# Tokens laid out by residue class in a decoder block: the dilated attention groups read side by side, the dense group regroups its blocks

## The chip, the cores and the metric

The kernel runs on one core of a Trainium2 chip. Its engines are TensorE (PE; its weight loads are listed as PEld), VectorE (DVE), ScalarE (ACT), GpSimd (POOL) and SyncE (SP), which issues most DMAs. Each engine works through its own instructions in program order. The metric is the device time of one execution in microseconds (us); the kernel before has a median of 969.9 us over three runs (968.4 to 971.77).

## The reference

One decoder block on 512 tokens of width 1024, in float32. `mod` comes from a condition vector `c` through `w_ada` (9216 outputs).

```python
u = modulate(rmsnorm(h, g_norm_ffn1), sh1, sc1)
h = h + 0.5 * gt1 * swiglu(u, w_ffn1_in, w_ffn1_out)
u = modulate(rmsnorm(h, g_norm_mix), sh2, sc2)
h = h + gt2 * token_mixing(u, ...)
u = modulate(rmsnorm(h, g_norm_ffn2), sh3, sc3)
h = h + 0.5 * gt3 * swiglu(u, w_ffn2_in, w_ffn2_out)
return rmsnorm(h, g_final)

def token_mixing(u, ...):
    p, q, k, v, gate_logits = split(u @ w_in)
    y_pool = multiscale_pool(p)      # trailing means over 2, 4, 8, 16 tokens, minus the token
    q, k = apply_rope(q), apply_rope(k)
    # three groups of 4 heads, head width 64: (window 128, dilation 1), (512, 4), (2048, 16);
    # token t attends to t - j * dilation, on banded blocks of 128 queries;
    # the groups are combined by a softmax over their log denominators
    y_attn = ...
    return (g_pool * (y_pool @ w_pool_branch) + g_attn * (y_attn @ w_attn_branch)) @ w_out
```

With dilation 4, tokens 4i + c for one c form a sequence of 128 that never meets the other three. Dilation 16 stays within the same class, with a mask (`(q - k) % 4 == 0`) inside it.

## The kernel before

All activations lie transposed: the 128 partitions hold features, the free dimension holds the 512 tokens, and a tensor of width 1024 is eight tiles of 128 x 512. Float32 products are made from three products of split operands: a weight chunk in `raw` (512 KB, loaded by SP, line 295) is rounded by ACT to `whi` (line 377), DVE makes the rest `wlo` (line 389), and the activations are kept as `UH` and `UL`. `take()` hands out split chunks, `split` and `look` make them ahead of use, and three `raw` buffers go round. `bg()` is work put between: one 128 x 1024 slice of `w_ada` in a buffer `xs` (loaded by SP, line 440) is multiplied with the condition and summed by DVE (line 448). It fetches up to two slices ahead, when it is called.

The change lies in `mix()`, the token mixing, from about 340 to 510 us of the span. The order on each engine is that in which the code is written; waits are set by the data. The steps, in their order:

1. q and k of group 0 (dilation 1) are made in four banks. `rope_two` copies them with signs (ACT, line 1409), moves 32-partition pieces with eight DMAs on SP (line 1412) and multiplies with the cosines (DVE, line 1414). `rope_b` adds the part with the sines (lines 1419, 1420).
2. v of group 0: four blocks n of 128 tokens, 24 matmuls each (lines 1675 to 1677), copied by ACT to `v1` (line 1678). Between them stand a weight split, its next load, `rope_b` and `bg()`. With n = 2 one `bg()` is called, with n = 3 two.
3. q and k of groups 1 and 2: eight `mm_tile`s of 24 matmuls (lines 421 to 423). At k = 5 of each stand, on PE, attention steps for group 0: the values (line 1508), the transposes of the probabilities (line 1490, `at_turn`) of the tile before, and new scores (line 1457). `at_exp` takes the scores with a mask and a maximum on DVE (lines 1473, 1475) and the exponential on ACT (line 1478). `rope_a` writes q and k of these groups sorted by class (`(i c) -> p c i`): DVE reads the bank and the cosines with a step of four elements (line 1402), `rope_b` reads the sine part so (line 1420).
4. Two tiles for the pooling mixer; `pool_diff` works them on POOL (lines 1583 to 1592).
5. v of groups 1 and 2, by class c: 24 matmuls of 128 tokens of the class against 512 columns. `by_class` gathers the class's columns of `UH` into `uc` or `v1` (ACT, line 1720); of `UL` the stationary operand is read with a step of four (line 1768). DVE copies the bank to `v23` (line 1769); the values of the dilated blocks (line 1508) read it.
6. The statistics of the dilated groups go through DRAM (`at_swap`, lines 1518, 1519) to the order of group 0; `at_merge`, `at_fT` and the rest combine the groups.

The functions that the diff touches, with the line numbers of the profile:

Of the kernel before, what the change touches and what calls it, by code (L numbers as in the profile page):

```python
# [14 lines left out]
P = 128  # L15
T = 512
# [149 lines left out]
class Kernel:  # L166
# [1226 lines left out]
    def rope_a(self, bank, dst, hp, classes, t, w):  # L1393


        nc = self.nc
        nc.scalar.activation(t, bank, AF.Copy, scale=self.sign)
# [4 lines left out]
        nc.vector.tensor_tensor(dst[:, hp * T:hp * T + T].rearrange("p (c i) -> p c i", c=classes), by(bank), by(self.cos),  # L1402
                                op=OP.mult)

    def rope_two(self, banks, dst, t, w):

        nc = self.nc
        for hp in range(2):
            nc.scalar.activation(t[:, hp * T:hp * T + T], banks[hp], AF.Copy, scale=self.sign)
        for i in range(4):  # L1410
            o = i ^ 1
            nc.sync.dma_start(w[32 * o:32 * o + 32], t[32 * i:32 * i + 32])
# [3 lines left out]
    def rope_b(self, dst, hp, classes, w):  # L1416
        v = self.nc.vector
        d = dst[:, hp * T:hp * T + T].rearrange("p (c i) -> p c i", c=classes)
        v.tensor_tensor(w, w, self.sin, op=OP.mult)
        v.tensor_tensor(d, d, w.rearrange("p (i c) -> p c i", c=classes), op=OP.add)  # L1420
# [17 lines left out]
    def at_tokens(self, u):  # L1438
        kind, n, hp = u
        return (1, 2) if kind else (0,), slice(n * P, n * P + P)  # L1440

    def at_scores(self, u):


        kind, n, hp = u
        nc = self.nc
        gs, toks = self.at_tokens(u)
        for i, g in enumerate(gs):
            for h in range(2):
                rows = slice(64 * h, 64 * h + 64)  # L1450
                q, k = (x[g][rows, hp * T:hp * T + T] for x in (self.qt, self.kt))
                if kind:
                    o, ks = slice(i * P, i * P + P), toks
                else:
                    o, ks = (slice(0, 2 * P), slice((n - 1) * P, (n + 1) * P)) if n else (slice(P, 2 * P), toks)
                S = self.bS[h][:, 2 * P * hp:2 * P * hp + 2 * P]
                nc.tensor.matmul(S[:, o], q[:, toks], k[:, ks], start=True, stop=True, skip_group_check=True)
# [41 lines left out]
    def at_values(self, u):  # L1499

        kind, n, hp = u
        pt = self.probT.pop(u)
        first = 0 if kind or n else 1
        for j in range(first, 2):
            for h in range(2):
                hc = 64 * (2 * hp + h)
                x = self.v23[:, n, 256 * j + hc:256 * j + hc + 64] if kind else self.v1[:, n - 1 + j, hc:hc + 64]
                self.nc.tensor.matmul(self.bO[64 * h:64 * h + 64, P * hp:P * hp + P], x,
                                      pt[:, (2 * h + j) * P:(2 * h + j + 1) * P], start=j == first, stop=j == 1,
                                      skip_group_check=True)  # L1510
        if hp == 1:
            o = self.o23.rearrange("p a (i c) -> p a c i", c=4)[:, :, n] if kind else self.o1[:, :, n * P:n * P + P]
            self.nc.vector.tensor_copy(o, self.bO[:, :256].rearrange("p (a i) -> p a i", a=2))

    def at_swap(self):

        nc = self.nc
        nc.sync.dma_start(self.scr.rearrange("(i c) f -> i c f", c=4), self.st)
        nc.sync.dma_start(self.stn, self.scr.rearrange("(n i) f -> i n f", n=4))
# [19 lines left out]
    def at_fT(self, bank):  # L1539
# [5 lines left out]
        nc.scalar.activation(self.fT[:8], bank[:8], AF.Copy)  # L1545
        v.tensor_tensor(self.fT[32:40], bank[:8], self.fT[:8], op=OP.subtract)
# [21 lines left out]
    def pool_diff(self, t, bank):  # L1568
# [8 lines left out]
        nc.scalar.activation(p[:, 16:], bank, AF.Copy)  # L1577
# [8 lines left out]
        for half, w in ((0, w0), (1, 2 * w0)):  # L1586
# [3 lines left out]
            g.tensor_scalar(d[rows, 16:], s[rows, 32:], 1.0 / w, None, op0=OP.mult)  # L1590
            g.tensor_tensor(d[rows, :16], s[rows, 16:32], ic, op=OP.mult)
            g.tensor_tensor(d[rows], d[rows], p[rows, 16:], op=OP.subtract)
# [17 lines left out]
    def mix(self):  # L1610
# [14 lines left out]
        with tc.tile_pool(name="rt", bufs=1) as self.rt, tc.tile_pool(name="aw", bufs=2) as self.aw:  # L1625
# [10 lines left out]
            masks = ma.tile([P, 3 * P], F32, name="masks")  # L1636
            nc.sync.dma_start(masks, self.a["cst"][:, 163:547])
            self.mask = [masks[:, :256], masks[:, 128:]]
# [25 lines left out]
            self.look(2)  # L1664
            for n in range(4):
# [7 lines left out]
                for k in range(KT):  # L1673
                    hi, lo = w[k]
                    M(b[:, :256], self.UH[k][:, ts], hi, start=k == 0, stop=False)
                    M(b[:, :256], self.UH[k][:, ts], lo, start=False, stop=False)
                    M(b[:, :256], self.UL[k][:, ts], hi, start=False, stop=k == KT - 1)
                nc.scalar.activation(self.v1[:, n, :], b[:, :256], AF.Copy)
                for i in ((), (0, 1), (2, 3), ())[n]:
                    self.rope_b(*to[i], 1, sw[i])  # L1680
# [22 lines left out]
            for g in (1, 2):  # L1703
                for dst in (self.qt[g], self.kt[g]):
                    for hp in range(2):
# [3 lines left out]
                        self.rope_a(b, dst, hp, 4, *rt)  # L1709

                        rest = [(6, lambda dst=dst, hp=hp, w=rt[1]: self.rope_b(dst, hp, 4, w))]
# [3 lines left out]
            uc = {}  # L1715

            def by_class(c):

                uc[c] = (ma if c % 2 else mp).tile([P, D], F32R, name="v1" if c % 2 else "uc")
                nc.scalar.activation(uc[c].rearrange("p (k i) -> p k i", k=KT),  # L1720
                                     self.UHv.rearrange("p (k i c) -> p c k i", k=KT, c=4)[:, c], AF.Copy)

            b = self.mm_tile(hooks([], rest + [(3, self.bg), (6, lambda: by_class(0))]))
# [15 lines left out]
            b = self.mm_tile(hooks(g23[0], [(2, lambda: by_class(1)), (3, u["copies"]), (4, u["adds"]), (7, self.bg)]))  # L1739
# [18 lines left out]
            for c in range(4):  # L1758
                mid = [lambda c=c: by_class(c + 1)] if c in (1, 2) else []
                hk = hooks(g23[c + 1] if c < 3 else [], [(k, f) for n, k, f in beside if n == c], mid)  # L1760
                b = self.nb()
                for k in range(KT):
                    for f in hk.get(k, ()):
                        f()
                    (hi, lo), uh = w[k], uc[c][:, k * P:k * P + P]
                    M(b, uh, hi, start=k == 0, stop=False)
                    M(b, uh, lo, start=False, stop=False)
                    M(b, self.UL[k][:, c::4], hi, start=False, stop=k == KT - 1)
# [368 lines left out]
def constants():  # L2137
# [4 lines left out]
    for t in range(2):  # L2142
        for half in range(2):
# [4 lines left out]
    q, k = i[:, None], i[None, :]  # L2148
    return np.concatenate([invf[i % 32][:, None], sign[:, None], np.zeros((P, 1), np.float32), cnt,
                           np.eye(P, dtype=np.float32),  # L2150
                           neg(k >= q), neg(k <= q), neg((k <= q) & ((q - k) % 4 == 0))], axis=1)


def lay_inputs(x, c, positions, w_ada, b_ada, g_norm_ffn1, w_ffn1_in, w_ffn1_out, g_norm_mix, w_in, w_pool,
# [7 lines left out]
    for g in range(4):  # L2162
# [3 lines left out]
        "xT": A(x)[0].T.reshape(KT, P, T).transpose(1, 0, 2).reshape(P, KT * T),  # L2166
        "c": A(c),
        "pos": A(positions),
# [25 lines left out]
```

## Time and profile before

| | |
|---|---|
| median of three runs | 969.9 us |
| span of the profiled execution, first to last instruction | 967.1 us |
| what lies around the span, median less span | 2.8 us |
| PE busy, of the span | 956.6 us (99%) |
| DVE, ACT, POOL busy | 846.8, 545.2, 82.8 us |
| mean granted TensorE clock | 0.998 |
| PE busy from 340 to 520 us | 179.60 of 180.00 us |

The 2.8 us hold the launch around a span and the difference between two executions. A timeline row gives start and duration in us from the span's start, then engine (SPq is SP issuing), line, operation, what is written and read, how many; in square brackets the idle time before it and what ended that. A row for a DMA tells how long SP took to issue, not how long the transfer took; its landing is told by the DMA view.

### The profile page before, as it was taken

To read this page: it belongs to the slowest core of one execution; us is meant where nothing else is said; L and a number is where in the kernel's file an instruction comes from. 1 tells how busy PE (TensorE), PEld (TensorE's weight loads), DVE (VectorE), ACT (ScalarE), POOL (GpSimd) and SP (SyncE) were. 2 spreads that over 40 slices of the span, in tenths; PEclk is the share of its full clock that TensorE was granted. 3 is DMA by queue.
4 is the path that set the end of the run, shared out by engine and by line. 5 is a ranking of instruction groups with operands and counts; after the bars stand their busy time and mean duration, and the time that the engine had idled before them with its cause. 6 is when DMAs were issued, how large, how long until landed. Compare 5 with 4: busy or idle time off the path is not lost.

```text
span 967.1 us, 18132 instructions
## 1 busy us (share of the span) xinstructions
PE 956.6 (99%) x7296; PEld 900.7 (93%) x7296; DVE 846.8 (88%) x1237; ACT 545.2 (56%) x817; POOL 82.8 (9%) x90
## 2 busy tenths in 40 slices
PE   9999999999999999999999999999999999999996
PEld 7888999999999899788899998998999999999996
DVE  7989999899999789898888777888899988989885
ACT  5443666665755553446665543465665657556565
POOL 0000110101010000006500000000001100010002
PEclk9999999999999999999999999999999999999999
DMA  9857785786768547767266537723757666665622
GB/s 354 282 179 256 187 246 159 201 213 153 218 175 254 167 145 226 247 192 221 54 163 186 133 108 231 243 63 111 181 153 194 163 167 175 163 165 136 179 69 88
DMA packets 53144, 174.12 MB, mean 180 GB/s; under 512 B 7105, under 2 KB 9921, under 8 KB 52802
## 3 DMA queue, kind: packets, MB, share of 16 engines
q1 hardware_dynamic: 43984, 141.23, 44.3%
q0 software_dynamic: 8496, 31.20, 17.9%
q8 instruction: 57, 0.93, 0.4%
q10 hardware_dynamic: 578, 0.53, 0.2%
q14 instruction: 29, 0.24, 0.1%
HBM read 135.29 MB, written 2.24 MB: 142 GB/s over the span
## 4 chain that ended last, share of the span: by engine, by line
PE 86%; DVE 8%; issue 2%; DMA 2%; ACT 1%; POOL 0%; POOLq 0%; ACTq 0%; DVEq 0%
PE bank L751 12%; PE bank L749 12%; PE bank L750 12%; PE bank L421 8%; PE bank L422 8%; PE bank L423 8%; PE bank L1110 4%; PE bank L1108 4%; PE bank L1109 4%; DVE wlo L389 2%; PE bank L2120 2%; PE bank L2124 2%; PE bank L2122 1%; DMA v<-wada 1%; DMA cs<-wada 1%
## 5 line engine op out<-in xcount | busy, mean ns | idle before, releaser
L389 DVE TENSOR_TENSOR wlo<-raw,whi 128x1024 fp32r<-128x1024 f32 (+3 forms) x150 | 166.0, 1115 | 35.0 <-ACT whi L377 34.9
L749 PE MATMUL bank<-UH,whi 128*128 128x256 f32 x672 | 185.5, 276 | 0.0
L750 PE MATMUL bank<-UL,whi 128*128 128x256 f32 x672 | 185.5, 276 | 0.0
L751 PE MATMUL bank<-UH,wlo 128*128 128x256 f32 x672 | 185.5, 276 | 0.0
L389 DVE TENSOR_TENSOR wlo<-X,whi 128x1024 fp32r<-128x1024 f32 (+3 forms) x133 | 142.0, 1080 | 17.6 <-ACT whi L377 17.5
L377 ACT ACTIVATE whi<-raw 128x1024 fp32r<-128x1024 f32 (+3 forms) x150 | 142.5, 963 | 21.2 <-DMA raw<-wf1o 7.8
L377 ACT ACTIVATE whi<-X 128x1024 fp32r<-128x1024 f32 (+3 forms) x133 | 123.1, 946 | 52.0 <-DVE X L312 46.8
L749 PEld LDWEIGHTS bank<-UH,whi 128*128 128x128 f32 x672 | 126.1, 188 | 0.1
L750 PEld LDWEIGHTS bank<-UL,whi 128*128 128x128 f32 x672 | 126.1, 188 | 0.0
L751 PEld LDWEIGHTS bank<-UH,wlo 128*128 128x128 f32 x672 | 126.1, 188 | 0.0
L749 PE MATMUL bank<-SH,whi 128*128 128x256 f32 x408 | 112.6, 276 | 0.0
L751 PE MATMUL bank<-SH,wlo 128*128 128x256 f32 x408 | 112.6, 276 | 0.0
L750 PE MATMUL bank<-SL,whi 128*128 128x256 f32 x408 | 112.6, 276 | 0.0
L421 PE MATMUL bank<-UH,whi 128*128 128x512 f32 (+1 forms) x272 | 92.9, 341 | 0.0
L422 PE MATMUL bank<-UL,whi 128*128 128x512 f32 (+1 forms) x272 | 91.8, 338 | 0.0
L423 PE MATMUL bank<-UH,wlo 128*128 128x512 f32 (+1 forms) x272 | 91.6, 337 | 0.0
L750 PEld LDWEIGHTS bank<-SL,whi 128*128 128x128 f32 x408 | 76.6, 188 | 0.0
L749 PEld LDWEIGHTS bank<-SH,whi 128*128 128x128 f32 x408 | 76.6, 188 | 0.0
L751 PEld LDWEIGHTS bank<-SH,wlo 128*128 128x128 f32 x408 | 76.6, 188 | 0.0
L1109 PE MATMUL bank<-HK,whi 128*128 128x256 f32 x224 | 61.8, 276 | 0.0
L1110 PE MATMUL bank<-HI,wlo 128*128 128x256 f32 x224 | 61.8, 276 | 0.0
L1108 PE MATMUL bank<-HI,whi 128*128 128x256 f32 x224 | 61.8, 276 | 0.0
(411 smaller groups left out, 2421.3 us busy)
## 6 DMA issues: line engine op xcount, KB each, us to landing
raw<-wmix SPq DMA_DIRECT2D x44, 512.0 KB, 4.2
raw<-wf1i SPq DMA_DIRECT2D x32, 512.0 KB, 5.8
raw<-wf2i SPq DMA_DIRECT2D x30, 512.0 KB, 4.3
ada<-wada SPq DMA_DIRECT2D x23, 512.0 KB, 5.6
X<-raw POOLq DMA_DIRECT2D x23, 512.0 KB, 6.0
xs<-wada SPq DMA_DIRECT2D x17, 512.0 KB, 5.3
X<-wf2i SPq DMA_DIRECT2D x14, 512.0 KB, 4.6
X<-wf1i SPq DMA_DIRECT2D x11, 512.0 KB, 4.5
```

What stands on the lines that cost most here:

```text
L377: self.nc.scalar.activation(self.hi[:, y], r[:, x], AF.Copy)
L389: self.nc.vector.tensor_tensor(self.lo[:, y], r[:, x], self.hi[:, y], op=OP.subtract)
L421: M(ps, hi, uh, start=start, stop=False)
L422: M(ps, hi, ul, start=False, stop=False)
L423: M(ps, lo, uh, start=False, stop=stop)
L749: M(o, hi, uh, start=start and p == 0 and k == 0, stop=False, skip_group_check=True)
L750: M(o, hi, ul, start=False, stop=False, skip_group_check=True)
L751: M(o, lo, uh, start=False, stop=k == 3, skip_group_check=True)
L1108: M(o, hi, uh, start=start and m % 2 == 0 and k == 0, stop=False, skip_group_check=True)
L1109: M(o, hi, ul, start=False, stop=False, skip_group_check=True)
L1110: M(o, lo, uh, start=False, stop=k == 1, skip_group_check=True)
L2120: M(b, hi, self.UH[k], start=k == 0, stop=False)
```

## The change

The host lays tokens in the order of class: position 128c + i holds token 4i + c, in `x`, in `positions` and, back again, in the result. Everything that is per token stays as it was. The dilated groups find their class as 128 neighbouring columns, so `rope_a`, `rope_b`, the class products and `o23` work on contiguous columns and `by_class` goes. What depends on token order has to undo the layout: group 0 writes q and k in blocks of 128 consecutive tokens, `(n c i)`, each block again sorted by class (new masks follow that order); its v is first copied to `vc` (in the buffer `uc`) and moved to `v1` by 16 DMAs of 32 partitions; its output, the statistics and the pooling mixer are reordered with access patterns.

```diff
-    def rope_a(self, bank, dst, hp, classes, t, w):
+    def rope_a(self, bank, dst, hp, t, w):
...
-        by = lambda x: x.rearrange("p (i c) -> p c i", c=classes)
-        nc.vector.tensor_tensor(dst[:, hp * T:hp * T + T].rearrange("p (c i) -> p c i", c=classes), by(bank), by(self.cos),
-                                op=OP.mult)
+        nc.vector.tensor_tensor(dst[:, hp * T:hp * T + T], bank, self.cos, op=OP.mult)
...
         for hp in range(2):          # rope_two
-            nc.vector.tensor_tensor(dst[:, hp * T:hp * T + T], banks[hp], self.cos, op=OP.mult)
+            by = lambda x: x.rearrange("p (c n i) -> p n c i", c=4, n=4)
+            o = dst[:, hp * T:hp * T + T].rearrange("p (n c i) -> p n c i", n=4, c=4)
+            nc.vector.tensor_tensor(o, by(banks[hp]), by(self.cos), op=OP.mult)
...
+    def rope_b(self, dst, hp, w, near=False):
         v.tensor_tensor(w, w, self.sin, op=OP.mult)
+        if near:
+            d = d.rearrange("p (n c i) -> p n c i", n=4, c=4)
+            w = w.rearrange("p (c n i) -> p n c i", c=4, n=4)
+        v.tensor_tensor(d, d, w, op=OP.add)
...
+            if kind:                 # at_values
+                self.nc.vector.tensor_copy(self.o23[:, :, n * P:n * P + P], b.rearrange("p (a i) -> p a i", a=2))
+            else:
+                self.nc.vector.tensor_copy(self.o1.rearrange("p a (c n i) -> p n a c i", c=4, n=4)[:, n],
+                                           b.rearrange("p (a c i) -> p a c i", a=2, c=4))
...
-        nc.sync.dma_start(self.scr.rearrange("(i c) f -> i c f", c=4), self.st)
-        nc.sync.dma_start(self.stn, self.scr.rearrange("(n i) f -> i n f", n=4))
+        nc.sync.dma_start(self.scr.rearrange("(c i) f -> i c f", c=4), self.st)
+        for c in range(4):
+            nc.sync.dma_start(self.stn[32 * c:32 * c + 32], self.scr.rearrange("(c n i) f -> c i n f", c=4, n=4)[c])
...
-        nc.scalar.activation(p[:, 16:], bank, AF.Copy)          # pool_diff
+        nc.scalar.activation(p[:, 16:].rearrange("p (i c) -> p c i", c=4), bank.rearrange("p (c i) -> p c i", c=4), AF.Copy)
...
+            o, by = d[rows].rearrange("p (c i) -> p c i", c=4), lambda x: x.rearrange("p (i c) -> p c i", c=4)
+            g.tensor_scalar(o[:, :, 4:], by(s[rows, 32:]), 1.0 / w, None, op0=OP.mult)
+            g.tensor_tensor(o[:, :, :4], by(s[rows, 16:32]), by(ic), op=OP.mult)
+            g.tensor_tensor(o, o, by(p[rows, 16:]), op=OP.subtract)
...
+            vc = mp.tile([P, D], F32, name="uc")
             for n in range(4):
...
-                nc.scalar.activation(self.v1[:, n, :], b[:, :256], AF.Copy)
+                nc.scalar.activation(vc[:, n * 256:n * 256 + 256], b[:, :256], AF.Copy)
+                for i in range(4):
+                    nc.sync.dma_start(self.v1[32 * n:32 * n + 32, i, :], vc[32 * i:32 * i + 32, n * 256:n * 256 + 256])
                 for i in ((), (0, 1), (2, 3), ())[n]:
-                    self.rope_b(*to[i], 1, sw[i])
+                    self.rope_b(*to[i], sw[i], True)
...
-            def by_class(c):
-                uc[c] = (ma if c % 2 else mp).tile([P, D], F32R, name="v1" if c % 2 else "uc")
-                nc.scalar.activation(uc[c].rearrange("p (k i) -> p k i", k=KT),
-                                     self.UHv.rearrange("p (k i c) -> p c k i", k=KT, c=4)[:, c], AF.Copy)
...
-                    (hi, lo), uh = w[k], uc[c][:, k * P:k * P + P]
+                    (hi, lo), uh, ul = w[k], *(x[k][:, c * P:c * P + P] for x in (self.UH, self.UL))
                     M(b, uh, hi, start=k == 0, stop=False)
                     M(b, uh, lo, start=False, stop=False)
-                    M(b, self.UL[k][:, c::4], hi, start=False, stop=k == KT - 1)
+                    M(b, ul, hi, start=False, stop=k == KT - 1)
```

The number and order of the matmuls on PE stay the same. The instructions move at two places.

SP in step 2, from the last piece moves of `rope_two` to the first of `rope_a`: `xs` is a slice of `w_ada`, `raw` a weight chunk, `q`, `k` and `rt` are rope pieces. Before:

```order
L1412 DMA k_3518<-v_3520 32x1024 x4
L440 DMA xs<-wada 128x1024
L295 DMA raw_63<-wmix 128x1024
L295 DMA raw_64<-wmix 128x1024
L440 DMA xs<-wada 128x1024
L295 DMA raw_65<-wmix 128x1024
L440 DMA xs<-wada 128x1024 x3
L1400 DMA rt_3976<-tr 32x512 x4
```

Loads alone stand between the two groups of moves.

And the same stretch of SP after, with `v_3519` for `v1`:

```order
L1410 DMA k_3518<-v_3520 32x1024 x4
L440 DMA xs<-wada 128x1024
L1687 DMA v_3519<-uc 32x256 x4
L295 DMA raw_63<-wmix 128x1024
L1687 DMA v_3519<-uc 32x256 x4
L295 DMA raw_64<-wmix 128x1024
L1687 DMA v_3519<-uc 32x256 x4
L440 DMA xs<-wada 128x1024
L295 DMA raw_65<-wmix 128x1024
L1687 DMA v_3519<-uc 32x256 x4
L440 DMA xs<-wada 128x1024 x3
L1400 DMA rt_3993<-tr 32x512 x4
```

Twelve moves of `v1` pieces stand ahead of the second single `xs` load, eight ahead of the second `raw` load, sixteen ahead of the last three `xs` loads.

DVE at the same place does not change its order. From the last `rope_b` of group 0 to the first maxima of the scores, after:

```order
L1419 TENSOR_TENSOR k_3518<-k_3518,cs 128x512
L1423 TENSOR_TENSOR k_3516<-k_3516,k_3518 128x512
L448 SCALAR_TENSOR_TENSOR xs,mod<-xs,cond 128x1024
L389 TENSOR_TENSOR wlo<-raw_65,whi 128x1024
L448 SCALAR_TENSOR_TENSOR xs,mod<-xs,cond 128x1024
L459 TENSOR_TENSOR mod<-mod,vecs 128x8
L448 SCALAR_TENSOR_TENSOR xs,mod<-xs,cond 128x1024
L389 TENSOR_TENSOR wlo<-raw_63,whi 128x1024
L1472 ISA prob,m_3527<-bank_93,masks 128x128
L1472 ISA m_3527 128x1
```

Three products with slices of `w_ada` (line 448) stand ahead of the first maximum (line 1472, 1473 before); the third of them reads the slice of that second single `xs` load.

ACT loses the four gathers of `UH`. In steps 4 and 5, before:

```order
L377 ACTIVATE whi<-raw_65 128x1024
L1720 ACTIVATE uc<-UH 128x1024
L1577 ACTIVATE tr<-bank_91 128x512
L377 ACTIVATE whi<-raw_63 128x1024
L1720 ACTIVATE v_4443<-UH 128x1024
L1478 ACTIVATE prob,st<-prob,negmax 128x256 x4
```

Two of the four gathers stand here, each ahead of other work of ACT. After, in the same steps:

```order
L377 ACTIVATE whi<-raw_65 128x1024
L1582 ACTIVATE tr<-bank_91 128x4x128
L377 ACTIVATE whi<-raw_63 128x1024
L1477 ACTIVATE prob,st<-prob,negmax 128x256 x4
```

The copies into the pooling scratch (line 1577, now 1582) write with a step of four elements.

More of the change, by code (lines that the diff above doesn't have):

```diff
@@ L1446, in at_scores @@
         nc = self.nc
-        gs, toks = self.at_tokens(u)
-        for i, g in enumerate(gs):
+        here = slice(n * P, n * P + P)
+        for i, g in enumerate((1, 2) if kind else (0,)):
             for h in range(2):
@@ L1758, in mix @@
             for c in range(4):
-                mid = [lambda c=c: by_class(c + 1)] if c in (1, 2) else []
-                hk = hooks(g23[c + 1] if c < 3 else [], [(k, f) for n, k, f in beside if n == c], mid)
+                hk = hooks(g23[c + 1] if c < 3 else [], [(k, f) for n, k, f in beside if n == c])
                 b = self.nb()
```

59 lines of the change are left out of this document (27 added, 32 removed).

## The prediction

> **What bounds the kernel now.** I read the page first, then the busy time by stretches, and then the timelines of PE, DVE and SP around the change.
>
> ```profile
> PE 956.6 (99%) x7296; PEld 900.7 (93%) x7296; DVE 846.8 (88%) x1237; ACT 545.2 (56%) x817; POOL 82.8 (9%) x90
> ...
> 380.00:391.00 11.00, 11.00 (x60) 8.84 (x59) 10.77 (x25) 3.33 (x11) 0.00 (x0) 1.00 0.83 293
> ```
>
> PE is busy all the time, here for 11.00 of 11.00 us; after it stand PEld, DVE (10.77 us: nearly as full), ACT and POOL, the granted clock, the DMA share and GB/s. So work taken from DVE or ACT gains nothing by itself. The time falls only where a matmul gets quicker or where PE waits, and it rises at once where PE is made to wait. The view of waits gives PE's only wait of this change's own work:
>
> ```profile
> PEld bank L1508 <- DVE v L1769: 0.6, 1, 0.6
> ```
>
> This is 0.6 us near 477 us, for a copy of `v23` that DVE makes late. More important is where PE does not wait but has nothing to spare. These rows are the first attention step of group 0 on DVE, ACT and PE:
>
> ```profile
> 382.48 1.22 DVE L448 SCALAR_TENSOR_TENSOR xs<-xs,cond 128x1024 f32<-128x1024 f32 x1
> ...
> 384.76 1.22 DVE L448 SCALAR_TENSOR_TENSOR xs<-xs,cond 128x1024 f32<-128x1024 f32 x1
> ...
> 386.11 1.22 DVE L448 SCALAR_TENSOR_TENSOR xs<-xs,cond 128x1024 f32<-128x1024 f32 x1
> ...
> 387.25 1.22 DVE L389 TENSOR_TENSOR wlo<-raw,whi 128x1024 fp32r<-128x1024 f32 x1
> ...
> 388.39 0.28 DVE L1473 CUSTOM_DVE_ANT_0 prob<-bank,masks 128x128 f32<-128x128 f32 x1
> ```
> ```profile
> 390.30 0.39 ACT L1478 ACTIVATE prob<-prob,negmax 128x128 f32<-128x128 f32 x1
> ```
> ```profile
> 385.66 0.39 PE L421 MATMUL bank<-UH,whi 128*128 128x512 f32 x1
> ...
> 390.20 0.39 PE L423 MATMUL bank<-UH,wlo 128*128 128x512 f32 x1
> 390.44 0.72 PE L1490 MATMUL bank<-cst,prob 128*128 128x128 f32 x4
> 390.92 0.48 PE L421 MATMUL bank<-UH,whi 128*128 128x512 f32 x1
> ```
>
> DVE works without a gap from 382 us to the maxima at 388.39; ACT ends the last of the four exponentials at 390.69; PE takes up their transposes at 390.44, four of them until 390.92. The last transposes need the exponential of 390.69, so PE's reserve here is about zero. Whatever delays DVE before 388.39 delays PE by the same.
>
> **The change part by part.** *Moves of `v1`.* Sixteen DMAs come into SP's queue between loads. How SP stands there:
>
> ```profile
> 370.23 2.47 SPq L1412 DMA_DIRECT2D q<-v  x4
> ...
> 376.76 0.53 SPq L440 DMA_DIRECT2D xs<-wada  x1
> 377.38 2.88 SPq L295 DMA_DIRECT2D raw<-wmix  x2
> 380.31 0.42 SPq L440 DMA_DIRECT2D xs<-wada  x1
> 384.87 0.33 SPq L295 DMA_DIRECT2D raw<-wmix  x1
> 385.25 2.44 SPq L440 DMA_DIRECT2D xs<-wada  x3
> ```
>
> Four moves of 32 partitions took 2.47 us, 0.62 each, and from 376.76 to 377.38 a load also held SP for 0.62. The new order from 376.76 is: load of `xs`, four moves, `raw`, four moves, `raw`, four moves, load of `xs`. Fifteen places of 0.62 are 9.3 us, so the second `xs` load is issued at 386.06 instead of 380.31. The copies that these moves wait for are ready: this is the third of the four blocks,
>
> ```profile
> 378.18 0.38 ACT L1678 ACTIVATE v<-bank 128x256 f32<-128x256 f32 x1 [1.38 <-PE bank L1677]
> ```
>
> and its moves come up at 383.5. So SP itself sets the pace. That load is the slice which the third product reads, the one at 386.11: the two before it read slices that are loaded by 376.76. Its transfer:
>
> ```profile
> xs<-wada SPq DMA_DIRECT2D x1, 512.0 KB, 4.9
> ```
> ```profile
> DMA to landing us min/median/max: 3.8/5.1/5.5
> ```
>
> The first row is that load alone, 4.9 us from issue to landing; the second is of the seven `xs` loads from 366 to 392 us. It landed at 385.2, 0.9 before its use. Now it lands at 386.06 + 4.9 = 391.0, with 3.8 and 5.5 as bounds between 389.9 and 391.6. DVE stands from 386.11 to 391.0, so 4.9 us (3.8 to 5.5). Behind the waiting product are queued the split of line 389 and the maxima; ACT waits for these, PE for ACT. With no reserve PE stops for 4.9 us at 390.44. It doesn't get this back: it is the bound before and after.
>
> The other delayed loads cost nothing beside it. The second `raw` is issued 3 us later, its chunk is used several tiles on. The first `raw` is issued at 379.9 and lands by 385.4 even at 5.5; its split stands at 387.25, behind the stop. The last moves of `v1` are issued before 389.2; pieces behind big loads need 4.5 us to land,
>
> ```profile
> rt<-rt SPq DMA_DIRECT2D x16, 64.0 KB, 4.5
> ```
>
> so `v1` is whole at about 393.7, before its first values, one tile (6 us) after the transposes.
>
> *Class products on PE.* Reading `UL` with a step of four made its weight loads longer:
>
> ```profile
> L1766 PEld LDWEIGHTS bank<-whi,uc x16: 186/188/189, 448.4 to 473.2; 128*128 128x128 f32 x16
> ...
> L1768 PEld LDWEIGHTS bank<-whi,UL x32: 307/309/310, 448.8 to 481.7; 128*128 128x128 f32 x32
> ```
> ```profile
> 456.32 0.40 PE L1766 MATMUL bank<-whi,v 128*128 128x512 f32 x1
> ...
> 459.35 0.40 PE L1767 MATMUL bank<-wlo,v 128*128 128x512 f32 x1
> ```
>
> 309 ns against 188, but loads run beside matmuls. What counts is the pace: from 456.32 to 459.35 there are 13 steps, 0.233 us each, against (390.20 - 385.66)/20 = 0.227 in the plain tiles above. 96 matmuls times 0.006 us are 0.6 us gained on the path.
>
> *`by_class`.*
>
> ```profile
> L1720 ACT ACTIVATE v<-UH 128x1024 fp32r<-128x1024 f32 x2 | 4.1, 2072 | 0.0
> ```
>
> Four gathers of 2.07 us, 8.3 us of ACT, go. PE waits for none of them, so nothing.
>
> *Rope and copies on DVE.*
>
> ```profile
> L1402 DVE TENSOR_TENSOR q<-bank,cs 128x512 f32<-128x512 f32 x4 | 4.3, 1078 | 0.4 <-ACT tr L1397 0.4
> ...
> L1420 DVE TENSOR_TENSOR q<-q,rt 128x512 f32<-128x512 f32 x4 | 4.4, 1091 | 0.1
> ...
> L1420 DVE TENSOR_TENSOR q<-q,q 128x512 f32<-128x512 f32 x2 | 1.4, 692 | 0.1
> ```
>
> With a step of four 1.08 and 1.09 us, plain 0.69. Sixteen operations of groups 1 and 2 save 0.4 each, 6.3 us of DVE, beside a busy PE: nothing. Group 0 gets eight operations over runs of 32 elements: no row has them; between plain (0) and the step of four (+0.4 each) lie 0 to 3.2 us, I take 0, as runs of 32 are nearest to plain. They stand ahead of the stop and vanish in it; without the stop they would cost what they last, for want of reserve.
>
> *Pooling on POOL, statistics, masks.* POOL's last operations get reads with a step of four; here are the first of these, POOL's last one before the change and a split on DVE beside it:
>
> ```profile
> L1590 POOL TENSOR_SCALAR ev<-rt 64x496 f32<-64x496 f32 x4 | 7.6, 1896 | 0.3
> ...
> 468.37 2.23 POOL L1592 TENSOR_TENSOR ev<-ev,v 64x512 f32<-64x512 f32 x1
> ...
> 469.38 2.30 DVE L389 TENSOR_TENSOR wlo<-AR,whi 128x1024 fp32r<-128x1024 f32 x1
> ```
>
> By DVE's ratio 1.09/0.69 = 1.58 the 7.6 us would become 12, as an upper bound; lower bound no change. POOL ended at 470.6; at worst it reaches past 475. The cost is to DVE: the split beside POOL's work took 2.30 us where the same at 387.25 took 1.22. Up to three such operations stand before the late copy at 477, so PE's wait there goes to 0 (-0.6) or grows by 3 x 1.1 = 3.3; I leave it as it is, since quicker copies and longer overlap pull against each other. The statistics get three more DMAs and short pieces:
>
> ```profile
> 477.78 0.38 SPq L1519 DMA_DIRECT2D stn<-scr  x1
> ...
> 489.75 0.17 DVE L1527 TENSOR_TENSOR mm<-m,stn 128x16 f32<-128x16 f32 x1
> ```
>
> 12 us cover them, against 3 x 0.62. The masks are a third larger in one early load: nothing.
>
> The sum: +4.9 - 0.6 = +4.3 us. Against the profiled execution it is 967.1 + 4.3 = 971.4 of span; on the median, 2.8 above that span, 969.9 + 4.3 = 974.2.
>
> **The rivals.** *The load is hidden after all (not slower).* The price of a place in SP's queue decides. Issued singly a DMA held SP for 0.33 us (384.87). At 0.33 the load goes out at 376.76 + 15 x 0.33 = 381.7 and lands at 386.6: a stop of 0.5 us, 969.9 + 0.5 - 0.6 = 969.8, and with the wait at 477 gone 969.2. The stop stays under 3.5 us, and so the change within 0.3% (2.9 us, about what a measurement of this kernel can tell from no change), as long as a place costs under 0.53 us. For it: single issues are short. Against it: moves in a row took 0.62 in every group.
>
> *The stop also slows PE's clock.* The trace has both states:
>
> ```profile
> L2021 PE MATMUL bank<-H,ones x18: 274/275/275, 9.8 to 14.7; 128*128 128x128 f32 x18
> ...
> L2021 PE MATMUL bank<-ones x10: 421/421/580, 1.1 to 3.1; 128*128 128x128 f32 x10
> ```
> ```profile
> 960.00:963.50 3.50, 0.11 (x1) 0.00 (x0) 1.78 (x6) 0.38 (x1) 1.41 (x2) 0.88 0.72 241
> 963.50:967.00 3.50, 0.00 (x0) 0.00 (x0) 0.00 (x0) 0.00 (x0) 0.00 (x0) 0.50 0.19 64
> ```
>
> The first matmuls took 421 ns, those after 9.8 us 275. When PE had ended, the granted clock went to half: a mean of 0.88 over 3.5 us is 0.84 us at half, so it fell some 2.7 us after the last work. A stop of 4.9 us, broken only by four transposes, is longer than that. At the start the clock was slow from 1.1 us at least to 3.1 and at most to 9.8; half speed for 2.0 to 8.7 us costs 1.0 to 4.3 us. I take 2.1: 974.2 + 2.1 = 976.3. Against it: whether the fall has a fixed grid in time isn't shown, nor how little work holds the clock up. [...]
>
> *POOL's longer work makes DVE late at 477.* As priced above, up to +3.3: 974.2 + 2 = 976 for two operations.
>
> **How the numbers follow.** The stop without a slow clock 0.42, with it 0.28, hidden or mostly so 0.22, POOL 0.05, a gain from DVE and ACT that I don't see 0.03. Time 974.2; range 969.2 (the hidden load) to 978.5 (the stop with the dearest slow clock, 4.3). Slower: 0.35 of the first case's 0.42 (a stop under 3.5 us takes the rest), 0.28 and 0.05, so 0.68; same: 0.07 of the first and nearly all of the hidden load, 0.28; faster 0.04.
>
> **What would show it.** In the profile after: SP's row for the `xs` load at about 386 behind twelve moves of `v1`; a DVE row of line 448 with some 5 us idle, released by DMA `xs<-wada`; PE idle before line 1490 at 390.4 by as much; pace 0.227 in the class products; a granted clock under 1 between 390 and 400 for the second rival. I am wrong if the `xs` load lands by 387, if PE shows no gap at 390, or if the operations over runs of 32 are what holds DVE.

## The result, and the profile after

The changed kernel takes 974.18 us (median of six, 973.37 to 975.68) beside 969.01 us of the kernel before (968.13 to 971.77) in the same comparison: a ratio of 1.0054, 95% interval 1.0039 to 1.0068, so 5.2 us slower. The profiled execution has a span of 971.6 us against 967.1.

The page's line of busy times, of the changed kernel:

```profile
PE 957.5 (99%) x7296; PEld 899.5 (93%) x7296; DVE 840.5 (87%) x1237; ACT 539.0 (55%) x813; POOL 85.0 (9%) x90
```

DVE and ACT each have 6 us less to do, as the change intends, and the time rises all the same. Three stretches by windows (PE, PEld, DVE, ACT, POOL busy, then granted clock, DMA share, GB/s):

```profile
380.00:391.00 11.00, 11.00 (x60) 8.86 (x58) 7.05 (x12) 1.54 (x3) 0.00 (x0) 1.00 0.78 234
391.00:396.00 5.00, 2.17 (x7) 1.26 (x7) 4.49 (x16) 2.60 (x10) 0.00 (x0) 0.84 0.95 327
396.00:400.00 4.00, 4.00 (x16) 3.17 (x15) 3.15 (x5) 2.42 (x7) 0.00 (x0) 0.77 0.40 97
```

DVE, busy for 10.77 of 11 us before, is busy for 7.05 between 380 and 391. PE then has 2.17 of 5 us, and the granted clock is 0.84 and 0.77, where it was 1.00. The view of waits has two new entries for PE from 340 us on:

```profile
PE bank L1489 <- ACT prob L1477: 2.8, 1, 2.8
...
PE bank L1507 <- DVE v L1769: 2.0, 1, 2.0
```

The first starts on SP. Its timeline (start, time to issue):

```profile
377.07 0.53 SPq L440 DMA_DIRECT2D xs<-wada  x1
377.70 2.41 SPq L1687 DMA_DIRECT2D v<-uc  x4
380.21 0.53 SPq L295 DMA_DIRECT2D raw<-wmix  x1
380.83 2.41 SPq L1687 DMA_DIRECT2D v<-uc  x4
383.34 0.53 SPq L295 DMA_DIRECT2D raw<-wmix  x1
383.96 2.41 SPq L1687 DMA_DIRECT2D v<-uc  x4
386.41 0.58 SPq L440 DMA_DIRECT2D xs<-wada  x1
```

Fifteen places in 9.34 us, 0.62 each; the second `xs` load goes out at 386.41 instead of 380.31. DVE and PE behind it:

```profile
390.37 1.22 DVE L448 SCALAR_TENSOR_TENSOR xs<-xs,cond 128x1024 f32<-128x1024 f32 x1 [3.85 <-DMA xs<-wada]
```
```profile
390.78 0.39 PE L423 MATMUL bank<-UH,wlo 128*128 128x512 f32 x1
393.95 1.63 PE L1489 MATMUL bank<-cst,prob 128*128 128x128 f32 x4 [2.78 <-ACT prob L1477]
395.23 0.78 PE L421 MATMUL bank<-UH,whi 128*128 128x512 f32 x1
395.80 0.63 PE L422 MATMUL bank<-UL,whi 128*128 128x512 f32 x1
...
397.91 0.39 PE L421 MATMUL bank<-UH,whi 128*128 128x512 f32 x1
...
401.11 0.39 PE L423 MATMUL bank<-UH,wlo 128*128 128x512 f32 x1
```

The chain is load, product (DVE stood 3.85 us), split, maxima, exponentials, transposes. From 395.23 to 397.91 a matmul of 128x512 takes 0.63 us where it takes 0.39 otherwise, and one starts every 0.43 us instead of every 0.23: the half clock.

PE's matmuls are the same 7296 in both kernels, so the loss can be read as the slip of one and the same matmul between the two traces:

| the same matmul | before | after | slip | added here |
|---|---|---|---|---|
| last ahead of the stop | 390.20 | 390.78 | 0.58 | (from the first 22 us, another execution) |
| first behind the four transposes | 390.92 | 395.23 | 4.31 | stop: 3.7 |
| twenty further on | 395.60 | 401.11 | 5.51 | half clock: 1.2 |
| last ahead of the values near 480 | 477.41 | 482.48 | 5.07 | class products and the like: -0.44 |
| these values (line 1507) | 478.08 | 484.87 | 6.79 | wait for DVE: 1.7 |

That is 6.2 us from 390 to 485. Some 0.8 less from there to the start of the last matmul is no more than executions differ: that rest takes 480.9 to 482.4 us over all kernels profiled here. The end of the span, behind the last matmul, is shorter as well: 5.5 us against 7.0 before. So the spans differ by 4.5 us only (0.6 + 6.2 - 0.8 - 1.5). This end takes 5.5 us in all ten profiles of kernels with the new layout, and 5.9 and 6.6 in the two other kernels that are built on the kernel before; what sets it stays open.

The second wait is for DVE's last but one copy of `v23`. POOL and DVE ahead of it, in the changed kernel:

```profile
471.17 4.58 POOL L1596 TENSOR_SCALAR ev<-rt 64x496 f32<-64x496 f32 x1
...
476.15 2.40 POOL L1598 TENSOR_TENSOR ev<-ev,v 64x512 f32<-64x512 f32 x1
```
```profile
473.94 2.03 DVE L312 TENSOR_TENSOR cs<-raw,AR 128x1024 f32<-128x1024 f32 x1
...
477.08 2.56 DVE L1326 TENSOR_TENSOR xs<-UH,UL 128x1024 f32<-128x1024 f32 x1
```
```profile
482.48 0.39 PE L1768 MATMUL bank<-whi,UL 128*128 128x512 f32 x1
484.87 0.88 PE L1507 MATMUL bank<-probT,v 128*64 128x128 f32 x12 [2.00 <-DVE v L1769]
```

POOL ends at 478.55, 7.9 us later than before where PE slipped by 5; beside it two DVE operations that take 1.22 elsewhere take 2.03 and 2.56. Before it was one (2.30).

### The profile page after: what moved, and what is told of

Same layout as the page of the kernel before. It is cut to its first block, busy times and chain, and to the rows that moved or that the text cites. A ratio compares the mean times of both kernels' runs of the same rounds, so it can differ in the third digit from the quotient of the medians.

```text
span 971.6 us, 18157 instructions
## 1 busy us (share of the span) xinstructions
PE 957.5 (99%) x7296; PEld 899.5 (93%) x7296; DVE 840.5 (87%) x1237; ACT 539.0 (55%) x813; POOL 85.0 (9%) x90
## 4 chain that ended last, share of the span: by engine, by line
PE 85%; DVE 7%; DMA 2%; issue 2%; ACT 1%; SPq 1%; POOL 0%; POOLq 0%; DVEq 0%; ACTq 0%
PE bank L750 12%; PE bank L749 12%; PE bank L751 12%; PE bank L421 8%; PE bank L422 8%; PE bank L423 8%; PE bank L1108 4%; PE bank L1109 4%; PE bank L1110 4%; DVE wlo L389 2%; PE bank L2120 2%; PE bank L2124 1%; PE bank L2122 1%; DMA cs<-wada 1%; DMA H<-xT 1%
```

## The experiments

Two theories stood against each other for the stop. By the first it is SP's queue: twelve moves stand ahead of one load. By the second it is the moves' own traffic, or DVE's work in the new order. For the rest, the questions were whether the half clock follows from the stop, and whether the step of four on POOL makes the second wait. The stop below is the time from PE's last matmul ahead of the first transposes (the filler not counted) to its first behind them, less the 0.7 us of before; the clock's share is what the next twenty matmuls take above their 4.68 us of before; the wait is that of line 1507 near 482, less the 0.67 of before between its neighbours' starts.

| kernel | median us | ratio to before, 95% | stop | half clock | wait |
|---|---|---|---|---|---|
| changed kernel | 974.18 | 1.0054 (1.0039 to 1.0068) | 3.7 | 1.2 | 1.7 |
| moves on ACT | 976.66 | 1.0076 (1.0061 to 1.0090) | 5.3 | 2.4 | 1.8 |
| three slices ahead | 977.52 | 1.0089 (1.0071 to 1.0108) | 1.6, and two more | 0 | 1.6 |
| POOL without a step | 972.68 | 1.0034 (1.0021 to 1.0046) | 3.4 | 1.6 | -0.3 |
| filler on PE | 973.23 | 1.0038 (1.0025 to 1.0051) | 3.3 | 0 | 1.7 |
| before, with moves | 972.82 | 1.0045 (1.0030 to 1.0059) | 3.1 | 0.95 | 0 |
| moves on POOL | 970.01 | 1.0016 (1.0004 to 1.0027) | 0.3 | 0 | 1.9 |
| one load ahead | 974.65 | 1.0052 (1.0033 to 1.0072) | one tile later | there | 1.9 |
| before, with 32 half moves | 982.48 | 1.0151 (1.0136 to 1.0166) | 10.9 | 1.2 | 0 |
| half of the moves on SP | 970.63 | 1.0026 (1.0016 to 1.0035) | 0.7 | 0 | 1.9 |
| moves on POOL, POOL without a step | 968.12 | 0.9994 (0.9986 to 1.0002) | 0.7 | 0 | -0.2 |

**The moves alone, in the kernel before.**

```diff
+            vc = mp.tile([P, D], F32, name="uc")
...
                 nc.scalar.activation(self.v1[:, n, :], b[:, :256], AF.Copy)
+                for i in range(4):
+                    nc.sync.dma_start(vc[32 * n:32 * n + 32, i * 256:i * 256 + 256], self.v1[32 * i:32 * i + 32, n, :])
```

> The kernel before, with nothing of the new layout, and sixteen DMAs of 32 partitions of v1 put on SP at the places where the changed kernel has its moves; they go to a buffer that nobody reads. If SP's queue alone makes the stop: the second xs load is issued near 386 and lands near 390, PE stops 2.8 to 3 us at 390 with the slow exponentials' pace and the half clock behind it, and the time rises by 3.5 to 4.8 us over before, to 972.7 to 974. If the stop needs the changed kernel's DVE work (operations over runs of 32), before with the moves stays within 1 us of before. The wait of 2 us near 482 should not come, since POOL's work is that of before.

It took 972.82 us. Its SP timeline has the load behind twelve moves, and DVE waits:

```profile
385.84 0.58 SPq L440 DMA_DIRECT2D xs<-wada  x1
```
```profile
389.74 1.23 DVE L448 SCALAR_TENSOR_TENSOR xs<-xs,cond 128x1024 f32<-128x1024 f32 x1 [3.15 <-DMA xs<-wada]
```

Nothing of the new layout is in this kernel, and the stop and the half clock are there, without the second wait. The moves alone make the first part of the loss, with 4.1 us of stop and clock.

**Twice the places, the same bytes.** Each of those sixteen moves is cut into two of 128 columns.

```diff
-                    nc.sync.dma_start(vc[32 * n:32 * n + 32, i * 256:i * 256 + 256], self.v1[32 * i:32 * i + 32, n, :])
+                    for h in (0, 128):
+                        nc.sync.dma_start(vc[32 * n:32 * n + 32, i * 256 + h:i * 256 + h + 128], self.v1[32 * i:32 * i + 32, n, h:h + 128])
```

> The kernel before with 32 moves of half the width (128 columns) in place of the sixteen: the same bytes, twice the places in SP's queue. If the places make the time, twelve more of 0.6 us stand ahead of the xs load: it is issued 7.5 us later than with sixteen, at about 393.3, lands near 397.3, and PE stops about 10 us in all: 972.8 plus 7.5 is 980.3, or 979.5 to 982 with the half clock's share. If bytes or descriptors in flight make it, about as with sixteen: 972.5 to 974.

982.48 us, half a microsecond above the upper end of what the places were expected to give. SP's timeline, and PE's wait:

```profile
389.28 4.94 SPq L1682 DMA_DIRECT2D uc<-v  x8
394.26 0.58 SPq L440 DMA_DIRECT2D xs<-wada  x1
```
```profile
PE bank L1490 <- ACT prob L1478: 9.9, 1, 9.9
```

Eight half moves take 4.94 us, 0.62 each, where four wide ones of the run before took 2.41, 0.60 each: SP is paid by the place here, not by the byte. Twelve places more cost the stop 7.7 us more (10.9 against 3.1). The bytes as the cause are out. (Whether the number of packets grew with the places is not shown; the next run keeps the moves as they are and takes only SP's queue away.)

**The moves on other queues.** On POOL:

```diff
-                    nc.sync.dma_start(self.v1[32 * n:32 * n + 32, i, :], vc[32 * i:32 * i + 32, n * 256:n * 256 + 256])
+                    nc.gpsimd.dma_start(self.v1[32 * n:32 * n + 32, i, :], vc[32 * i:32 * i + 32, n * 256:n * 256 + 256])
```

> The changed kernel with the sixteen moves of v1 issued by POOL, which has no other work between 340 and 448 us. SP's order is that of before and ACT issues nothing. If it is the queue alone: the product at 386 finds its slice, no stop and no half clock, 969.4 to 970.2 (what stays is the wait near 482). Rivals: POOL takes some 0.9 us for one issue, 15 us in all, so v1 is whole only at about 392 to 394, in time for the values at 397, but if it is later than 397 PE waits there; and POOL's issuing may lengthen DVE's operations beside it, as POOL's operations do near 470, which would delay the maxima by 1 us or more: 970.5 to 973.

970.01 us. POOL's issues, DVE's product, and PE's wait that stays:

```profile
373.51 2.04 POOL L1687 DMA_DIRECT2D v<-uc  x4 [76.81 <-DMA q<-v]
```
```profile
386.43 1.23 DVE L448 SCALAR_TENSOR_TENSOR xs<-xs,cond 128x1024 f32<-128x1024 f32 x1 [0.44 <-DMA xs<-wada]
```
```profile
PE bank L1507 <- DVE v L1769: 2.1, 1, 2.1
```

The same moves with the same bytes, away from SP: the product waits 0.44 us instead of 3.85, PE's stop is 0.3 us, the clock stays whole. That settles the first theory. The traffic is not free all the same. The `xs` load, issued at 380.12, took 6.3 us to land beside these moves (6.5 in the other kernel that has them on POOL), where it took 4.9 before:

```profile
xs<-wada SPq DMA_DIRECT2D x1, 512.0 KB, 6.3
```

That uses up the 0.9 us which it had in reserve, and makes the 0.44 of waiting. DVE's operations beside POOL's issuing keep their 1.22 us, and an issue on POOL took 0.5 us, not the 0.9 of its 512 KB loads (line 320, 0.85 to 1.00).

On ACT (`nc.scalar.dma_start` at the same line):

> The sixteen moves of v1 are issued by ACT instead of SP; nothing else changes. If SP's queue is what makes the change slow, the second xs load goes out near 381 us as before, the product of line 448 waits for nothing, PE's gap of 2.8 us at 391 and the half clock behind it (another 1.3 us) go, and the time falls by 4.3 to 4.8 us, to 969.4 to 969.9. Rival one, the moves' own traffic or DVE's operations over runs of 32 elements hold the step: the gap stays, 973.5 to 974.5. Rival two, ACT becomes the late one: sixteen issues of 0.6 us are 9.6 us on ACT between 373 and 388, the exponentials at 390 come late and PE still stops for 1 to 3 us: 970.5 to 973.

976.66 us, worse than on SP. The second rival was right that ACT becomes the late one, but the time lies above its range, and the path is another: the `xs` load is late again. ACT, SP and DVE:

```profile
381.78 2.44 ACTq L1687 DMA_DIRECT2D v<-uc  x4
384.26 1.06 ACT L377 ACTIVATE whi<-raw 128x1024 fp32r<-128x1024 f32 x1 [2.52 <-DMA v<-uc]
```
```profile
373.82 6.72 SPq L1410 DMA_DIRECT2D k<-v  x4
...
384.86 0.81 SPq L295 DMA_DIRECT2D raw<-wmix  x2
385.72 0.42 SPq L440 DMA_DIRECT2D xs<-wada  x1
```
```profile
392.33 1.22 DVE L448 SCALAR_TENSOR_TENSOR xs<-xs,cond 128x1024 f32<-128x1024 f32 x1 [3.32 <-DMA xs<-wada]
```

Each of the first three fours holds ACT's own next split for 2.5 to 2.6 us. I read the rest from the order of these rows, and no run isolates it: the split frees its `raw` buffer late, SP stands at a `raw` load until 384.86, and the same `xs` load is late behind it, at 385.72. It then took 6.6 us to land. SP was late before that already: its last piece moves of k ended at 380.54 instead of 376.97, and why is not shown.

Every other move on POOL, eight left on SP:

```diff
+                    (nc.gpsimd, nc.sync)[i % 2].dma_start(self.v1[32 * n:32 * n + 32, i, :], ...)
```

> The changed kernel with every other move on POOL: eight stay on SP, six of them ahead of the xs load. By places of 0.62 us it is issued at 386.4 less 3.7, 382.7, lands at 386.7 to 387 and is used at 386.4: a stop of at most 0.5 us and no half clock, so 970.0 to 970.5, as with none on SP. If a smaller number already holds the step, for want of reserve on DVE behind it (the next three loads still come 5 us late), a stop near 404 instead: 971 to 973.

970.63 us. SP and DVE:

```profile
382.22 0.58 SPq L440 DMA_DIRECT2D xs<-wada  x1
```
```profile
387.36 1.23 DVE L448 SCALAR_TENSOR_TENSOR xs<-xs,cond 128x1024 f32<-128x1024 f32 x1 [0.59 <-DMA xs<-wada]
```

With six moves ahead instead of twelve the wait is 0.59 us instead of 3.85, and the clock stays whole in this profile: six moves were nearly free. Other executions differ: three of the eleven runs took 971.9 to 973.0 us at the lowest granted clocks of the eleven (0.996 and 0.997), so the half clock probably came there.

**The load ahead of the moves.** First by a fetch that runs three slices ahead everywhere (`self.ada_depth` 3 instead of 2):

> The moves stay on SP; the slices of w_ada are fetched three ahead instead of two (ada_depth 3), so the load that was late stands ahead of all twelve moves in SP's queue. If the place in the queue is the cause: the product at 386 us finds its slice, the stop and the slow clock go, 969.4 to 969.9. If the moves cost by their traffic, or by holding later loads (raw, the next three slices), 971 to 974. A second way to fail: the earlier load waits on a buffer that is not yet free and holds the rope pieces behind it in SP's queue; then q and k of group 0 come late and PE waits before the first scores at 384.

977.52 us, no better than on ACT. DVE at the first sines, and PE's waits:

```profile
378.09 0.69 DVE L1419 TENSOR_TENSOR q<-q,cs 128x512 f32<-128x512 f32 x1 [2.31 <-DMA q<-v]
```
```profile
PE bank L1489 <- ACT prob L1477: 4.1, 3, 1.8
```

What the second way to fail foresaw came, late pieces, but by another path: SP issues the rope pieces of q at 370.67 (370.81 in the changed kernel), so they are not held in its queue; with three loads in flight ahead of them instead of two they land 5.4 to 5.9 us after their issue instead of 2.4 to 3.9. DVE waits 2.31 us for them, and so it goes on in later tiles: three waits of up to 1.8 us on PE. Then with only the one load ahead:

```diff
+            self.ada_depth = 3
...
             self.bg()
             self.look(1)
             self.held = self.pos
+            self.ada_depth = 2
```

> The moves stay on SP; only the one load that was late (the second single xs load) is fetched one step earlier, right behind the load ahead of the moves. All other orders stay, unlike in the run with three ahead everywhere. If that load alone makes the stop, PE's gap at 391 goes (969.4 to 970). If DVE has no reserve behind the stop, the next products, whose loads still stand behind all sixteen moves (issued at 390, landed at 394 to 396), hold DVE instead at 391 to 394 and PE stops one step later, near 404: part of the gain is given back, 970.5 to 973.

974.65 us. DVE's next product, and PE's wait:

```profile
395.53 1.23 DVE L448 SCALAR_TENSOR_TENSOR xs<-xs,cond 128x1024 f32<-128x1024 f32 x1 [3.85 <-DMA xs<-wada]
```
```profile
PE bank L1489 <- ACT prob L1477: 2.0, 1, 2.0
```

The stop at 390 is gone, and the next load, behind all sixteen moves, makes the next product wait for 3.85 us. PE stops one tile later, until 408.2, and the half clock follows from 410.0. Two of the six runs kept a granted clock of 0.999 and 1.000, and took 969.74 and 972.85 us. So no single load is at fault: SP's queue is 10 us longer, and in this stretch DVE has a reader for each load.

**Filler in the stop.** Ten matmuls without use, ahead of the first transposes:

```diff
         blocks = (1, 3) if (kind == 0 and n == 0) else (0, 1, 2, 3)
+        for _ in range(10 if u == (0, 0, 0) else 0):
+            nc.tensor.matmul(b, self.UH[0][:, :P], self.UH[0], start=True, stop=True, skip_group_check=True)
```

> Ten matmuls of 128x512 without use (their bank is overwritten by the transposes) are put on PE ahead of the first transposes of group 0, so PE works through 2.3 us of the 2.8 us for which it stood. The stop's end is set by ACT and does not move. If the half clock from 394.4 to 397.9 came from the idle time before it, the granted clock stays at 1 and the time falls by 1.1 to 1.3 us, to 972.9 to 973.1. If the slow rows after the stop are only PE pacing itself by the exponentials, nothing changes: 974.0 to 974.4. If the clock falls anyway, and the filler overshoots the stop, 974.2 to 975.

973.23 us, 0.95 below the changed kernel. PE, and the window from 391 to 396:

```profile
392.37 2.43 PE L1489 MATMUL bank<-UH 128*128 128x512 f32 x10
```
```profile
391.00:396.00 5.00, 4.78 (x20) 3.23 (x18) 4.16 (x14) 1.64 (x9) 0.00 (x0) 1.00 0.88 309
```

PE does useless work in place of none, the granted clock is 1.00 instead of 0.84, and the next twenty matmuls take the 4.68 us of before: the idle time was the cause of the half clock, worth 1.2 us in the trace. The intervals of the two ratios overlap, but the granted clocks do not: 0.998 to 1.000 in the six runs here, 0.995 to 0.997 in the six of the changed kernel.

**The pooling mixer without a step.** POOL works in token order; the mixer's four products read the result with a step of four.

```diff
-            g.tensor_scalar(o[:, :, 4:], by(s[rows, 32:]), 1.0 / w, None, op0=OP.mult)
-            g.tensor_tensor(o[:, :, :4], by(s[rows, 16:32]), by(ic), op=OP.mult)
-            g.tensor_tensor(o, o, by(p[rows, 16:]), op=OP.subtract)
+            g.tensor_scalar(d[rows, 16:], s[rows, 32:], 1.0 / w, None, op0=OP.mult)
+            g.tensor_tensor(d[rows, :16], s[rows, 16:32], ic, op=OP.mult)
+            g.tensor_tensor(d[rows], d[rows], p[rows, 16:], op=OP.subtract)
...
-                                 self.pd[t][rows], start=True, stop=True, skip_group_check=True)
+                                 self.pd[t][rows].rearrange("p (i c) -> p c i", c=4), start=True, stop=True, ...)
```

> The pooling mixer's last operations on POOL (lines 1596 to 1598) read and write without a step, in token order; the four matmuls that use the result read it with a step of four instead. The stop at 391 stays. If the strided operations of POOL are what makes DVE late near 482 us, PE's wait there falls from 2.0 us to the 0.3 to 0.6 of before: 972.4 to 972.9. If the wait comes only from how POOL and DVE happen to meet, POOL's times and the wait change little: 973.7 to 974.5. If matmuls pay for the strided reading, less than 1 us is added near 504.

972.68 us. POOL's end, DVE, and the products that read with a step:

```profile
471.99 2.72 POOL L1597 TENSOR_TENSOR ev<-ev,v 64x512 f32<-64x512 f32 x1
```
```profile
476.85 1.21 DVE L1326 TENSOR_TENSOR xs<-UH,UL 128x1024 f32<-128x1024 f32 x1
```
```profile
502.49 2.01 PE L1608 MATMUL bank<-ev,wpool 64*64 64x512 f32 x8
```

POOL ends 3.8 us earlier, DVE's operation at 477 is no longer stretched, and the wait is gone. But the matmuls pay 0.9 us for the step (2.01 against 1.09), so the trace gains less than the wait.

**The class products.** `UL` is read with a step of four again (`self.UL[k][:, c::4]`).

> The changed kernel, in which the class products read UL again with a step of four (the columns are then other tokens', so these products are not those of the reference). Only the weight loads of line 1768 change, 188 to about 309 ns. If the step costs pace, as the 0.233 against 0.227 us per matmul suggested, the 96 matmuls take 0.3 to 0.6 us longer, over those of the changed kernel; if the loads were hidden, the pace stays 0.227 and before's slower pace came from elsewhere.

One run of 975.97 us, in whose trace the half clock lasted twice as long (a mean granted clock of 0.995, 0.996 in the changed kernel's trace). Its weight loads:

```profile
L1768 PEld LDWEIGHTS bank<-whi,UL 128*128 128x128 f32 x32 | 9.9, 309 | 1.5
```

Over the 91 steps from one class product to the next, PE takes 21.55 us before, 21.22 in the changed kernel and 21.55 here. So the step costs 0.33 us and not more.

**Both causes away.** Moves on POOL, POOL without a step, and the order of the mixer undone by ACT and DVE as they copy its banks:

```diff
-            nc.scalar.activation(self.PH[r], b, AF.Copy, scale=sc)
-            nc.vector.scalar_tensor_tensor(self.PL[r], b, sc, self.PH[r], op0=OP.mult, op1=OP.subtract)
+            h, l = (x[r].rearrange("p (c i) -> p c i", c=4) for x in (self.PH, self.PL))
+            b = b.rearrange("p (i c) -> p c i", c=4)
+            nc.scalar.activation(h, b, AF.Copy, scale=sc)
+            nc.vector.scalar_tensor_tensor(l, b, sc, h, op0=OP.mult, op1=OP.subtract)
```

> Both causes taken away: the moves of v1 on POOL's queue (as in the run that gave 970.0), and the pooling mixer on POOL without a step, its order undone where ACT and DVE copy the mixer's banks instead of on PE. If the stop and the wait near 482 were the whole loss, 970.0 less 1.7 is 968.3, which is before's 969.0 less what the class products gain (0.3) and the like: 968.0 to 969.0, not to be told from before. If the two contend (POOL now has both works) or the copies of the banks with a step hold PE near 505, 969.3 to 970.5.

968.12 us, ratio 0.9994 (0.9986 to 1.0002). The class values follow the last matmul ahead of them after 0.50 us, and the mixer's products take 1.09 us again:

```profile
479.52 0.39 PE L1769 MATMUL bank<-whi,UL 128*128 128x512 f32 x1
480.02 1.10 PE L1507 MATMUL bank<-probT,v 128*64 128x128 f32 x16
...
499.21 1.09 PE L1608 MATMUL bank<-ev,wpool 64*64 64x512 f32 x8
```

The new layout then costs nothing, and gains nothing that can be told from before either. Two causes, the moves in SP's queue and the step on POOL, account for the whole loss as far as these medians can tell.

## Why the prediction was right, and where it was not

The time (974.2 foreseen, 974.18 measured) and the sign came out, but the sum behind them was only partly right.

- *The late load.* Right in mechanism and nearly in size. The load was issued at 386.41 (386.06 foreseen), the product waited for it, and PE stood ahead of the transposes. The place in the queue, 0.62 us, held; the rival with 0.33 us fell, and the run with half moves shows the price by itself. The transfer took 3.9 us, near its lower bound of 3.8, so the stop was 3.7 us instead of 4.9.
- *The slow clock.* It was a rival with a chance of 0.28, and it happened: 1.2 us, below the 2.1 taken. PE had stood for 2.78 us until 393.95, and the clock fell at 394.45, among the four transposes behind. (At the end of the trace before, the prediction reads 2.7 us from the last work to the fall; its rows give 2.6, from 960.11 to 962.66.) The step that failed is the choice of the likeliest case, a stop that leaves the clock alone; stop and clock together are 4.9 us, the figure that had been given to the stop alone.
- *POOL.* The step that failed most. The term was set to 0 with a bound of 3.3, and as a case it had a chance of 0.05; it cost 1.7. The bound's reasoning was right (POOL slows more of DVE's long operations: two instead of one, of the three that it allowed), the choice within it was not. POOL's unhurried multiplication grew by a third, not by 1.58:

```profile
L1590 POOL TENSOR_SCALAR ev<-rt x4: 1451/1892/2348, 445.8 to 463.9; 64x496 f32<-64x496 f32 x4
...
L1596 POOL TENSOR_SCALAR ev<-rt x4: 1915/1930/4578, 451.8 to 471.2; 64x496 f32<-64x496 f32 x4
```

  The shortest of four was 1451 ns before (line 1590) and is 1915 now, 1.32 times as long, with reads at a step of four elements; in the run without the step on POOL the shortest is 1.45 us again. POOL and DVE were stretched side by side: DVE's operations at 473.94 and 477.08 took 2.03 and 2.56 us for 1.22, POOL's multiplication beside the first 4.58 for 1.92, and its subtraction beside the second 2.40 for 1.55. What lengthens them is not shown.
- *Class products.* Right in sign, 0.33 us (0.44 with all that lies between) for a foreseen 0.6; the pace fell to 0.227 as said.
- *What was costed at nothing.* `by_class`, the rope operations and the DMAs of the statistics cost or gained nothing that shows. The open one, DVE's operations over runs of 32 elements, was taken at 0 and is 0:

```profile
L1414 DVE TENSOR_TENSOR q<-bank,cs 128x512 f32<-128x512 f32 x2 | 1.3, 686 | 0.1
```

- *The sum.* 3.7 + 1.2 + 1.7 - 0.4 is 6.2 us in the two traces and 5.2 by the medians, where 4.3 was foreseen. That the time agrees to 0.1 us is luck: the sum was 0.9 too small and stood on a median of before that was 0.9 above that of the six runs. Two of the three rivals came true on top of the likeliest case; at their own prices (2.1 and 2) they would have made it 978.3.

## What to carry to other kernels

Count a new DMA as a place in its queue (0.62 us on SP here), not by its bytes: find what stands behind it and whether an engine waits for that, and if there is an idle queue, put it there (POOL's here, 970.01 us for 974.18); an engine with work of its own (ACT here, 2.5 us for four) pays the issues in its own stream. Freed time on engines that are not the bound gained nothing (6 us each on DVE and ACT here), while a wait on the bound costs itself and, where the clock falls behind it, another 1.0 to 2.4 us in these runs. Where an operation on POOL gets longer, look at which DVE operations it now lies beside (1.22 us became 2.03 and 2.56 here), not at POOL's own time.

## What the runs showed of the hardware

- In the changed kernel's trace the half clock lasts from 394.45 to 397.86, 3.41 us at a granted clock of 0.50. The whole clock ahead of it begins at 5.33 and lasts 389.12 us, 114 times 3.413; the one behind it lasts until 967.89, 570.03 us, 167 times. In the trace of the kernel before the whole clock lasts from 6.93 to 962.66, 955.73 us, 280 times. So in these two executions the clock changed after whole multiples of 3.41 us, counted from a start that is not the same in both. From the last matmul to the last fall it was 2.6 us in the one and 1.8 in the other (966.06 to 967.89).
- In the 3.41 us ahead of the half clock PE was busy for 0.57 us. With the ten matmuls in the stop it was busy for 4.78 of 5.00 us from 391 to 396, and the clock stayed whole. With the 32 half moves it was busy for 1.12 of 11 us from 391 to 402, and the granted clock was 0.94 from 391 to 396, 0.50 to 402 and 0.70 to 408: some 10.2 us of half clock. How much work is enough to hold the clock up is not shown. The price of a like stop differs: 0.95 to 1.6 us in the three rows of the table with a stop of 3.1 to 3.7 us and half clock behind it.
- An issue of a DMA of 32 partitions, in a row of four or eight, held SP for 0.60 to 0.62 us, with 128 columns as with 256 (4.94 us for eight, 2.41 for four), and ACT for 0.61 to 0.64 (2.44 to 2.56 for four); on POOL it took about 0.5 (1.96 to 2.04 for four).
- With the moving operand read at a step of four elements, eight float32 products of 64x512 took 2.01 us on PE instead of 1.09. With the weights read so, a load took 309 ns instead of 188, of which 0.33 us in 91 steps reached the path.
